# Raw weight tiles in a pool of their own, in the place of later token sums, and one more staging tile

## The chip, the cores and the metric

One core of one Trainium2 chip runs the whole step. The metric is the device time of one execution in microseconds (us). Before the change it is 3220.15 us, the median of two runs (3218.65 and 3221.65).

## The reference

One layer of a streaming encoder, for a prompt of 2048 tokens and a sample of 32 tokens, width 1024. A row-normalised input is multiplied by `w_in` (1024 by 9760), whose columns are cut into attention q, k, v and its gate, the state-space parts z, x, B, C and dt, and two merge gates:

```python
h = _rms_norm(x, pre_norm_w)
proj = h @ w_in
q, k, v, g_att, z, xbc, dt_raw, gate_a, gate_s = _split_cols(proj)
# windowed attention over q, k, v -> att; conv, SiLU and chunked scan over xbc, dt, z -> yz
branch_a = (att * jax.nn.silu(g_att)) @ w_attn_o
branch_s = yz @ w_ssm_o
merged = jax.nn.sigmoid(gate_a) * branch_a + jax.nn.sigmoid(gate_s) * branch_s
out = merged @ w_out
return x + _rms_norm(out, post_norm_w), ...
```

All of it is float32. The returned values are the two outputs and the new caches and states.

## The kernel before

**Tokens and precision.** The prompt is worked in four blocks of 512 tokens; the sample rides along in block 1 (544 columns). A float32 product is made from two halves of each operand in a shorter format: a weight `w` is split into a high part (ScalarE, L142) and a remainder (VectorE, L143), and likewise the tokens, and three products hi·hi, hi·lo, lo·hi are accumulated on TensorE (`group`, L178).

**Weights.** A weight tile holds 512 rows by 128 columns. In block 0 it comes raw from its matrix (`load_raws`, L121, 256 KB) into a pool of `NR` = 4 tiles, is split by `alloc` into one of nine `w` tiles (1 + 1 instructions of ScalarE and VectorE), and the split pair is stored to a scratch tensor `wd` (L147, 512 KB). Blocks 1 to 3 load the split pair from there (L131). `supply` runs `alloc` up to eight entries ahead of TensorE's use. A raw tile may be loaded again when `rawdone` has been moved on, which happens in `alloc` by `en["free"]` tiles at a time.

**Jobs.** A job is a pair of 128-column outputs. For the columns of x, B, C and z ("plain" pairs) block 0 makes four weight tiles and each frees its raw tile by itself. The pairs of k, v, q, the attention gate and the two merge gates ("fast" pairs, in this order: K, V, q0, g0, q1, g1, the fourth part of the state-space output, q2, g2, q3, g3, four of gate S, four of gate A) use seven products instead of eight in blocks 1 to 3. For that, block 0 makes four sums of the raw tiles on GpSimd (L136, each written over one of its inputs), splits and stores them too, although block 0 itself doesn't multiply by them. So a fast pair in block 0 has four raw tiles, eight splits and seven stores, and `free` is 0 for all of it but the last sum, which frees all four raw tiles at once. Behind the fast pairs come the attention output (ao, 8 jobs) and the output matrix (ou, 8 jobs).

**Running a job in block 0.** `emit_both` (L236 on) runs 24 matmuls for each of the two output halves into the two banks of one PSUM tile, then copies the half to a staging tile (L251, mostly `xq`, two buffers, of ScalarE's work). In the built program the first matmul of the second half waits for the copy of the first half.

**What sets the order.** The code is recorded in the order of its calls, and a scheduler with its own time estimates then orders each engine's instructions; every engine, SP's DMA queue too, works its list strictly in order. SP issues the kernel's DMAs: raw loads (L121), stores (L147), loads of split weights (L131), x (L369), z to and from scratch (L570, L696) and the scan's decay rows (L600, L603).

**Token sums.** The tiles t2, t3 and t4 (operands of the seven products) are first written by `sums_c`, at the end of block 0 for block 1. Before the change they stand in the pool `hp` from the start of the program.

Of the kernel before, what the change touches and what calls it, by code (L numbers as in the profile page):

```python
# [7 lines left out]
F32 = mybir.dt.float32  # L8
F32R = mybir.dt.float32r
# [5 lines left out]
P = 128  # L15
# [7 lines left out]
HK = KT // 2  # L23
# [4 lines left out]
C_Z, C_X, C_DT, C_GA, C_GS = 2560, 4608, 7680, 7712, 8736  # L28
CUT = object()
NW = 9  # L30
NR = 4


@with_exitstack
def hybrid_step_kernel(ctx: ExitStack, tc: tile.TileContext, ins, outs):
# [4 lines left out]
    pool = lambda n, b, **k: ctx.enter_context(tc.tile_pool(name=n, bufs=b, **k))  # L40
    const = pool("const", 1)
    wp = pool("wp", NW)
    hp = pool("hp", 1)
    up = pool("up", 2)
    sp = pool("sp", 8)
    s2 = pool("s2", 6)
    xq = pool("xq", 2)
    sm = pool("sm", 4)
    dram = pool("dram", 2, space=bass.MemoryType.DRAM)
    wdram = pool("wdram", 1, space=bass.MemoryType.DRAM)  # L50
# [24 lines left out]
    cdec = const.tile([P, 160], F32, name="cdec")  # L75
    HN = UW // 2
    hb = {n: hp.tile([P, 2, HK, UW], F32R, name=n) for n in ("h1", "h2")}
    hb.update({n: hp.tile([P, 2, HK, HN], F32R, name=n) for n in ("t2", "t3", "t4")})
    HOME = {"b11": ("h1", 0), "b12": ("h1", 1), "t1": ("h1", 1), "b21": ("h2", 0), "b22": ("h2", 1),
            "t2": ("t2", 0), "t3": ("t3", 0), "t4": ("t4", 0)}  # L80

# [27 lines left out]
    rawlist = []  # L109
    rawtiles = {}  # L110
    rawnext, rawdone = [0], [0]
# [4 lines left out]
    def load_raws():  # L116
        while rawnext[0] < min(len(rawlist), rawdone[0] + NR):
            i = rawnext[0]
            view, k0, c0 = rawlist[i]
            r = wp.tile([P, HK * P], F32, name="raw", bufs=NR)  # L120
            dma(r.rearrange("p (k c) -> p k c", k=HK), view[:, k0:k0 + HK, c0:c0 + P])  # L121
            rawtiles[i] = r
            rawnext[0] += 1

    def alloc(e):
        en = entries[e]
        w = slots[e] = wp.tile([P, 2, HK * P], F32R, name="w")
        mix = en["kind"] == "mix"
        if en["load"]:
            n = 1 if mix else 2  # L130
            dma(w[:, :n].bitcast(F32), held[en["key"]])  # L131
            return
        r = rawtiles[en["raw"]]
        if en.get("sum"):
            dst, x, y, op = en["sum"]
            pl.tensor_tensor(*(rawtiles[en["raw0"] + i] for i in (dst, x, y)), op=op)  # L136
        if mix:
            r, h = (t.rearrange("p (k c) -> p k c", k=HK) for t in (r, w[:, 0]))
            act.activation(h, r, AF.Copy)
            vec.tensor_tensor(h[:, :, 32:64], r[:, :, :32], h[:, :, :32].bitcast(F32), op=ALU.subtract)  # L140
        else:
            act.activation(w[:, 0], r, AF.Copy)  # L142
            vec.tensor_tensor(w[:, 1], r, w[:, 0].bitcast(F32), op=ALU.subtract)  # L143
        if en["keep"]:
            u = w[:, :1] if mix else w
            held[en["key"]] = wdram.tile([P, u.shape[1], HK * P], F32, name=f"wd{e}")
            dma(held[en["key"]], u.bitcast(F32))  # L147
        rawdone[0] += en["free"]
        load_raws()
# [194 lines left out]
    def block(b):  # L344
# [13 lines left out]
        def stage_a(io):  # L358
# [31 lines left out]
            def raw(name):  # L390
                j, half = dict(b11=(0, 0), b12=(0, 1), b21=(1, 0), b22=(1, 1))[name]
                return st["rawh"][j][:, :, half * (tb // 2):(half + 1) * (tb // 2)]

            def parts(name, src):
                o = operand(name, tb // 2)
                act.activation(o[:, 0], raw(src), AF.Copy)
                vec.tensor_tensor(o[:, 1], raw(src), o[:, 0].bitcast(F32), op=ALU.subtract)

            def to(dst, x, y):
                vec.tensor_tensor(raw(dst), raw(x), raw(y), op=ALU.subtract)  # L400
# [15 lines left out]
                    dma(st["t1d"][:, :, k, :nh], t[:, :, :nh].bitcast(F32))  # L416

            def sums_c():
                to("b21", "b21", "b22")
                parts("t3", "b12")  # L420
                parts("t2", "b22")
                parts("t4", "b21")
# [852 lines left out]
    for slot in blocks[0]["stage_a"](ph):  # L1275
        for f in slot:
            f()

    load_raws()
    par = const.tile([P, 208], F32, name="par")  # L1280
    convw = par[:, :96].rearrange("p (t n) -> p t n", t=4)
# [137 lines left out]

    if phase:  # L1420
        phase.pop("cm").__exit__(None, None, None)


_INS = ['x_prompt', 'x_sample', 'cache_k', 'cache_v', 'state_conv', 'state_ssm', 'pre_norm_w', 'w_in', 'conv_w', 'conv_b',
# [47 lines left out]
```

## Time and profile before

| | |
|---|---|
| median of two runs | 3220.15 us |
| the profiled execution | 3225.96 us |
| its span, first to last instruction | 3224.2 us |
| TensorE (PE) busy in it | 3009.6 us, 93% |
| VectorE (DVE) / ScalarE (ACT) / GpSimd (POOL) busy | 60% / 38% / 19% |
| DMA, mean share of 16 engines | 72.6% |
| TensorE's mean granted clock | 0.973 of full speed |

The profile lists instructions by source line. "Idle before, releaser" is the time an engine stood before an instruction and what ended it. A granted clock of 1.0 is 2.4 GHz and 0.5 is 1.2 GHz; a value between them is a mix over the stretch. A busy TensorE can be a slow one, so clock and busy time are read together.

### The profile page before, as it was taken

The page shows a single profiled execution, that of the slowest core. Times are in us where ns is not written, and L with a number is a line of the kernel's source. Part 1 is how long each engine was busy: PE and PEld are TensorE (multiplying, and loading weights), DVE is VectorE, ACT ScalarE, POOL GpSimd, SP SyncE. Part 2 cuts the span into 40 slices and gives each one's busy share as a digit, 9 for nine tenths or more (in the row PEclk, how much of TensorE's full clock was granted, in tenths as well). Part 3 has the DMA queues.
Part 4 walks back from the last instruction along what each step waited for, and adds up shares of the span by engine and source line. Part 5 has one row for each costly group of instructions (what it writes and reads, how often), then busy time and mean ns, then how long its engine had stood idle before and what let it go on. Part 6 is the DMA issues. An engine that isn't in the chain of part 4 may idle for free.

```text
span 3224.2 us, 51384 instructions
## 1 busy us (share of the span) xinstructions
PE 3009.6 (93%) x19007; PEld 2570.8 (80%) x19007; DVE 1935.7 (60%) x3965; ACT 1227.0 (38%) x2942; POOL 617.3 (19%) x698
## 2 busy tenths in 40 slices
PE   7999978887999999899999998999999999999998
PEld 6777756666899899888998777788888777788887
DVE  7788856764566666556345665556536575655622
ACT  5565434553444542124224444214313444313411
POOL 1233232322113322100011232210010222210000
PEclk9999988898999999999999999999999999999999
DMA  8888866577976676766867776686887667686794
GB/s 293 296 279 273 270 231 243 211 258 283 310 226 213 183 211 191 262 206 192 305 218 216 216 214 201 219 303 184 269 279 232 212 209 212 206 295 213 223 324 140
DMA packets 430947, 767.39 MB, mean 238 GB/s; under 512 B 35848, under 2 KB 259432, under 8 KB 430696
## 3 DMA queue, kind: packets, MB, share of 16 engines
q1 hardware_dynamic: 430696, 764.10, 72.6%
q8 instruction: 151, 2.47, 0.3%
q14 instruction: 100, 0.82, 0.1%
HBM read 587.19 MB, written 176.80 MB: 237 GB/s over the span
## 4 chain that ended last, share of the span: by engine, by line
PE 61%; DVE 12%; DMA 10%; ACT 6%; POOL 5%; issue 5%; SPq 1%; DVEq 0%; POOLq 0%; ACTq 0%
PE mm L178 51%; DMA rr<-cd 4%; POOL raw L136 2%; ACT rr L628 2%; DVE u L552 2%; DVE w L143 2%; DMA raw<-in_w_in_dram 2%; PE sd L933 1%; PE sd L659 1%; POOL rr L625 1%; PE sd L976 1%; PE sd L655 1%; PE sd L959 1%; DMA s<-zd 1%; PE sd L663 1%
## 5 line engine op out<-in xcount | busy, mean ns | idle before, releaser
L178 PE MATMUL mm<-h,w 128*128 128x512 f32 (+2 forms) x8336 | 1602.4, 346 | 104.7 <-ACT xq L251 54.6
L178 PEld LDWEIGHTS mm<-h,w 128*128 128x128 f32 x8336 | 1317.3, 193 | 324.4 <-ACT xq L251 69.3
L178 PE MATMUL mm<-v,w 128*128 128x512 f32 (+1 forms) x2400 | 487.6, 356 | 9.3 <-ACT w L142 3.7
L178 PEld LDWEIGHTS mm<-v,w 128*128 128x128 f32 x2400 | 393.3, 190 | 79.3 <-ACT w L142 4.6
L143 DVE TENSOR_TENSOR w<-raw,w 128x512 fp32r<-128x512 f32 x288 | 238.0, 841 | 96.6 <-ACT w L142 91.9
L178 PE MATMUL mm<-t,w 128*128 128x256 f32 (+1 forms) x1944 | 271.2, 287 | 0.0
L178 PEld LDWEIGHTS mm<-t,w 128*128 128x128 f32 x1944 | 249.2, 190 | 4.4 <-issue 4.3
L142 ACT ACTIVATE w<-raw 128x512 fp32r<-128x512 f32 x288 | 174.6, 627 | 157.8 <-POOL raw L136 79.6
L628 ACT ACTIVATE rr<-rr,ncum 128x128 f32<-128x128 f32 (+1 forms) x544 | 168.7, 385 | 131.7 <-POOL rr L625 131.7
L251 ACT COPY xq<-mm 128x512 f32<-128x512 f32 (+1 forms) x226 | 110.9, 508 | 232.1 <-PE mm L178 231.8
L552 DVE SCALAR_TENSOR_TENSOR u<-xq,par,u 128x512 f32<-128x512 f32 x192 | 157.8, 822 | 37.6 <-ACT u L543 36.4
L178 PE MATMUL mm<-tA,w 128*128 128x512 f32 (+2 forms) x688 | 174.6, 341 | 0.0
L914 ACT ACTIVATE pt<-sd,nm 128x192 f32<-128x192 f32 (+3 forms) x260 | 104.9, 412 | 162.2 <-DVE nm L908 157.3
L625 POOL TENSOR_SCALAR_AFFINE_SELECT rr<-rr 128x1024 f32<-128x1024 f32 (+1 forms) x68 | 87.6, 1289 | 338.8 <-DMA rr<-cd 278.4
L814 POOL TENSOR_TENSOR s<-s,cs 128x512 f32<-128x512 f32 (+1 forms) x40 | 63.9, 1606 | 454.6 <-DVE s L812 330.8
L136 POOL TENSOR_TENSOR raw<-raw 128x512 f32<-128x512 f32 x72 | 104.3, 1448 | 199.7 <-DVE w L143 195.6
L178 PEld LDWEIGHTS mm<-tA,w 128*128 128x128 f32 x688 | 118.3, 188 | 13.7 <-ACT v L1083 0.2
L178 PE MATMUL mm<-S,w 128*128 128x512 f32 (+2 forms) x344 | 115.9, 337 | 0.1
L906 DVE TENSOR_REDUCE mx<-sd 128x2 f32<-128x384 f32 (+3 forms) x140 | 66.0, 510 | 82.9 <-PE sd L933 78.2
L645 DVE SCALAR_TENSOR_TENSOR rr<-rr,sd 128x1024 f32<-128x1024 f32 (+1 forms) x68 | 79.3, 1165 | 53.0 <-ACT rr L628 53.0
L639 POOL TENSOR_TENSOR s<-xd,te 128x512 f32<-128x512 f32 (+1 forms) x68 | 76.4, 1124 | 163.1 <-DVE xd L636 163.1
L644 POOL TENSOR_TENSOR xl<-s,xh 128x512 fp32r<-128x512 f32 (+1 forms) x68 | 92.2, 1358 | 80.3 <-ACT xh L643 79.5
(274 smaller groups left out, 3788.4 us busy)
## 6 DMA issues: line engine op xcount, KB each, us to landing
w<-wd SPq DMA_DIRECT2D x810, 512.0 KB
wd<-w SPq DMA_DIRECT2D x270, 512.0 KB
raw<-in_w_in_dram SPq DMA_DIRECT2D x154, 256.0 KB
rr<-cd SPq DMA_DIRECT2D x64, 512.0 KB
ee<-cd SPq DMA_DIRECT2D x128, 128.0 KB
x<-in_x_prompt_dram SPq DMA_DIRECT2D x24, 512.0 KB
zd<-xq SPq DMA_DIRECT2D x48, 256.0 KB
s<-zd SPq DMA_DIRECT2D x48, 256.0 KB
```

The source lines that it names most:

```text
L136: pl.tensor_tensor(*(rawtiles[en["raw0"] + i] for i in (dst, x, y)), op=op)
L142: act.activation(w[:, 0], r, AF.Copy)
L143: vec.tensor_tensor(w[:, 1], r, w[:, 0].bitcast(F32), op=ALU.subtract)
L178: last_mm[0] = pe.matmul(ps, a[:, k, :], r(k, n0, n), start=start and k == 0 and i == 0, stop=stop and k == HK - 1 and i == len(ops) - 1)
L251: act.copy(y[:, n0:n0 + n], ps)
L552: vec.scalar_tensor_tensor(o[:, d0:d0 + n], src[:, t:t + n], convw[:, t, ci:ci + 1], o[:, d0:d0 + n], op0=ALU.mult, op1=ALU.add)
L625: pl.affine_select(w[:q, :, :q], w[:q, :, :q], pattern=[[0, 8], [1, q]], compare_op=ALU.is_ge, fill=-1e30, base=0, channel_multiplier=-1)
L628: act.activation(w[:q, h, :q], w[:q, h, :q], AF.Exp, scale=1.0, bias=ncum[:q, co + g * 8 + h:co + g * 8 + h + 1])
L639: pl.tensor_tensor(xe[:q].rearrange("p (h d) -> p h d", h=8), xd[:q], te[:q, hs].unsqueeze(2).broadcast_to([q, 8, 64]), op=ALU.mult)
L644: pl.tensor_tensor(xl[:q], xe[:q], xh[:q].bitcast(F32), op=ALU.subtract)
L645: vec.scalar_tensor_tensor(w[:q, :, :q], w[:q, :, :q], 0.25, pb[:q, P:P + q].unsqueeze(1).broadcast_to([q, 8, q]), op0=ALU.mult, op1=ALU.mult)
L914: act.activation(dst, src, AF.Exp, bias=nm[:, i:i + 1], scale=0.125, accum_out=den[:, i:i + 1])
```

## The change

The raw tiles get a pool of their own, `early`, with `NR` = 12 buffers, at the other end of the on-chip memory ("right"). `open_sums`, called at the head of `sums_c`, closes it when the last raw tile has been used and opens the pool `late` in its place, which holds t2, t3 and t4. The staging pool `xq` goes from two to three buffers. No instruction of the computation is added or removed.

```diff
-NR = 4
+NR = 12
...
-    xq = pool("xq", 2)
+    xq = pool("xq", 3)
+    early_cm = tc.tile_pool(name="early", bufs=NR, side="right")
+    early = early_cm.__enter__()
...
-    hb.update({n: hp.tile([P, 2, HK, HN], F32R, name=n) for n in ("t2", "t3", "t4")})
+    late_cm = []
+
+    def open_sums():
+        if not late_cm:
+            assert rawnext[0] == rawdone[0] == len(rawlist)
+            early_cm.__exit__(None, None, None)
+            late_cm.append(tc.tile_pool(name="late", bufs=1, side="right"))
+            p = late_cm[0].__enter__()
+            hb.update({n: p.tile([P, 2, HK, HN], F32R, name=n) for n in ("t2", "t3", "t4")})
...
         while rawnext[0] < min(len(rawlist), rawdone[0] + NR):
             i = rawnext[0]
             view, k0, c0 = rawlist[i]
-            r = wp.tile([P, HK * P], F32, name="raw", bufs=NR)
+            r = early.tile([P, HK * P], F32, name="raw")
...
             def sums_c():
+                open_sums()
                 to("b21", "b21", "b22")
...
     if phase:
         phase.pop("cm").__exit__(None, None, None)
+    late_cm[0].__exit__(None, None, None)
```

The scheduler lays block 0 out anew; behind the first part of block 1 every engine's list is the one of before. In the rows below numbers behind a name are those of single buffers, and line numbers of the changed kernel are up to twelve higher (L121 is L131 there, L142 is L152, L251 is L261, L782 is L793, L147 is L157, L369 is L379).

On ScalarE, in the pairs of gate A, before: `mm_6677` is the PSUM tile of one pair, `w_6596`, `w_6601`, `w_6633` and `w_6636` are its four weight tiles, and the four `w` rows behind them are splits of its sums.

```order
L142 ACTIVATE w_6596<-raw_6555 128x512
L142 ACTIVATE w_6601<-raw_6557 128x512
L142 ACTIVATE w_6633<-raw_6559 128x512
L142 ACTIVATE w_6636<-raw_6561 128x512
L370 ACTIVATE xn_7445,ss_7446<-x_7444 128x1024
L142 ACTIVATE w_6641<-raw_6561 128x512
L142 ACTIVATE w_6647<-raw_6559 128x512
L142 ACTIVATE w_6653<-raw_6555 128x512
L142 ACTIVATE w_6659<-raw_6557 128x512
L251 COPY xq_6676<-mm_6677 128x512
L782 ACTIVATE tA_6713<-xq_6676 128x512
L251 COPY xq_6676<-mm_6677 128x512
```

The same place after the change: `mm_6693` is the PSUM tile of a pair, and the raw tiles 6465 to 6471 are those of the pair behind it.

```order
L152 ACTIVATE w_6718<-raw_6465 128x512
L793 ACTIVATE tA_6690<-xq_6586 128x512
L152 ACTIVATE w_6723<-raw_6467 128x512
L152 ACTIVATE w_6755<-raw_6469 128x512
L261 COPY xq_6692<-mm_6693 128x512
L152 ACTIVATE w_6758<-raw_6471 128x512
L793 ACTIVATE tA_6729<-xq_6692 128x512
L152 ACTIVATE w_6763<-raw_6471 128x512
L152 ACTIVATE w_6769<-raw_6469 128x512
L152 ACTIVATE w_6775<-raw_6465 128x512
L152 ACTIVATE w_6781<-raw_6467 128x512
L261 COPY xq_6692<-mm_6693 128x512
```

Before, all eight splits of a pair stood ahead of that pair's two copies; now the eight splits between a pair's copies belong to the next pair, and three of them stand ahead of the first copy, one and then four behind it.

On SP, at the same pairs, before: the loads of x for block 1 (L369) stand among the raw loads.

```order
L121 DMA raw<-in_w_in_dram 128x4x128 x4
L369 DMA x<-in_x_prompt_dram 128x1024
L147 DMA wd_6705<-w 128x1024
L147 DMA wd_6710<-w 128x1024
L147 DMA wd_6745<-w 128x1024
L147 DMA wd_6751<-w 128x1024
L147 DMA wd_6757<-w 128x1024
L147 DMA wd_6763<-w 128x1024
L147 DMA wd_6769<-w 128x1024
L121 DMA raw<-in_w_in_dram 128x4x128 x4
```

After, x is loaded at the end of block 0, among the last stores of the output matrix:

```order
L131 DMA raw<-in_w_out_dram 128x4x128
L157 DMA wd_7320<-w 128x1024
L157 DMA wd_7325<-w 128x1024
L157 DMA wd_7362<-w 128x1024
L157 DMA wd_7367<-w 128x1024
L375 DMA nw<-in_pre_norm_w_dram 128x1024
L379 DMA x<-in_x_prompt_dram 128x1024
L157 DMA wd_7439<-w 128x1024
L157 DMA wd_7444<-w 128x1024
L379 DMA x<-in_x_prompt_dram 128x1024
```

Five loads of x and one of the norm's weights have moved from the fast pairs to behind all raw loads, eight stores from the end of block 0. On TensorE the five groups of transposes that need them stood ahead of matmuls 1, 25, 49, 73 and 151 of the 192 of the output matrix, and now stand behind 120, 142, 153, 170 and 190 of them. At the program's start SP issues twelve raw loads instead of four ahead of the small constants.

## Rows read from the trace of the kernel before

**Rows 1.** Busy time by stretch: us, each engine, granted clock (PEclk), DMA share, GB/s.

```profile
50.00:403.00 353.00, 338.25 (x1738) 270.93 (x1736) 290.06 (x469) 192.53 (x410) 102.64 (x106) 0.99 0.85 280
403.00:429.00 26.00, 24.03 (x108) 18.35 (x108) 13.84 (x28) 7.81 (x13) 9.13 (x8) 1.00 0.65 225
429.00:516.00 87.00, 60.31 (x197) 44.43 (x198) 46.29 (x61) 29.58 (x53) 31.07 (x22) 0.82 0.63 227
516.00:683.00 167.00, 150.13 (x848) 108.07 (x846) 125.44 (x297) 93.70 (x278) 48.85 (x32) 0.93 0.63 230
683.00:785.00 102.00, 77.13 (x273) 57.41 (x269) 49.66 (x72) 40.59 (x70) 29.65 (x22) 0.87 0.75 269
785.00:882.00 97.00, 97.00 (x454) 79.39 (x454) 54.57 (x99) 42.38 (x74) 15.61 (x11) 1.00 0.92 315
882.00:3224.20 2342.20, 2229.65 (x15257) 1965.21 (x15255) 1321.09 (x2853) 794.09 (x2001) 376.87 (x480) 0.98 0.71 227
```

**Rows 2.** What TensorE waited for from 403 to 785 us: total, times, longest.

```profile
PE mm L178 <- ACT xq L251: 27.2, 10, 5.5
PE mm L178 <- ACT w L142: 20.0, 13, 2.3
PE mm L178 <- DVE w L143: 5.4, 2, 2.7
```

**Rows 3.** TensorE in order of time: start, length, instructions, [idle before and releaser].

```profile
726.70 6.08 PE L178 MATMUL mm<-h,w 128*128 128x512 f32 x24 [1.85 <-ACT w L142]
736.52 7.13 PE L178 MATMUL mm<-h,w 128*128 128x512 f32 x24 [3.74 <-ACT xq L251]
745.51 0.74 PE L178 MATMUL mm<-h,w 128*128 128x512 f32 x2 [1.85 <-ACT w L142]
```

**Rows 4.** ScalarE in the same stretch, in order of time.

```profile
726.03 2.18 ACT L142 ACTIVATE w<-raw 128x512 fp32r<-128x512 f32 x4
...
735.37 0.63 ACT L142 ACTIVATE w<-raw 128x512 fp32r<-128x512 f32 x1 [1.04 <-POOL raw L136]
735.90 0.57 ACT L251 COPY xq<-mm 128x512 f32<-128x512 f32 x1
```

**Rows 5.** SP's DMA issues in the same stretch, in order of time.

```profile
727.39 9.67 SPq L147 DMA_DIRECT2D wd<-w  x7
737.16 2.90 SPq L121 DMA_DIRECT2D raw<-in_w_in_dram  x4
```

**Rows 6.** Two short stretches of the cycle before, columns as in Rows 1.

```profile
718.00:725.00 7.00, 6.84 (x23) 5.08 (x21) 2.03 (x6) 0.18 (x2) 0.00 (x0) 0.76 1.04 329
725.50:728.00 2.50, 1.30 (x5) 0.80 (x6) 1.33 (x3) 2.50 (x5) 0.00 (x0) 1.00 0.05 18
```

**Rows 7.** The page's DMA issues: count and size of each.

```profile
wd<-w SPq DMA_DIRECT2D x270, 512.0 KB
raw<-in_w_in_dram SPq DMA_DIRECT2D x154, 256.0 KB
```

**Rows 8.** TensorE in the attention output's jobs, unbroken and at full clock.

```profile
799.08 2.95 PE L178 MATMUL mm<-u,w 128*128 128x512 f32 x12
801.87 2.95 PE L178 MATMUL mm<-v,w 128*128 128x512 f32 x12
```

**Rows 9.** VectorE: four splits without and four with GpSimd's sums beside them.

```profile
726.67 2.50 DVE L143 TENSOR_TENSOR w<-raw,w 128x512 fp32r<-128x512 f32 x4 [6.47 <-ACT w L142]
...
731.30 5.42 DVE L143 TENSOR_TENSOR w<-raw,w 128x512 fp32r<-128x512 f32 x4 [0.49 <-ACT w L142]
```

**Rows 10.** TensorE's waits from 882 us to the end, first row.

```profile
PE mm L178 <- ACT xq L251: 25.3, 15, 3.9
```

**Rows 11.** GpSimd's waits from 882 us to the end, for a staging tile.

```profile
POOL xq L541 <- DMA zd<-xq: 24.5, 7, 6.0
```

**Rows 12.** SP's queue at the start: the last small constant.

```profile
15.73 0.43 SPq L63 DMA_DIRECT2D dbc<-in_d_skip_dram  x1
```

**Rows 13.** TensorE at the start: the first use of a small constant.

```profile
28.91 0.27 PE L1302 MATMUL sd<-cst,s 120*128 120x120 f32 x1
```

## What I predicted, before the result was known

> **What bounds the kernel now.** I read the busy times by stretch first, since a share over the whole program hides where time is lost. In [rows 1] TensorE is all but full nearly everywhere: 338 of 353 us up to the fast pairs, 97 of 97 us in the jobs behind them, 2230 of 2342 us in blocks 1 to 3. The hole is at the fast pairs of block 0: from 429 to 516 us it works 60 of 87 us at a clock of 0.82, from 683 to 785 us 77 of 102 us at 0.87. Between them, where attention runs beside the pairs, it works 150 of 167 us at 0.93. No other engine is full there, and the DMA engines are busy 0.63 to 0.75 of the time. So a chain of waits, and no engine, sets the pace.
>
> The list of waits names it [rows 2]: TensorE waits for the copies out of PSUM (L251, 27.2 us) and for splits of weights (L142 and L143, 25.4 us). One cycle in order of time shows why. A first half starts at 726.70, the second at 736.52, the next pair's first at 745.51 [rows 3]: 18.8 us a pair. The four splits that the first half needs start at 726.03, so only then were the raw tiles there [rows 4]. Then come the sums on GpSimd, whose last split starts at 735.37, and only behind it stands the copy of the first half, at 735.90, while that half had ended at 732.8: 3.7 us lost. The four raw loads of the next pair stand on SP behind all seven stores, at 737.16 [rows 5], because the last sum frees all four raw tiles at once. They land while TensorE runs its second half, and 1.85 us are lost again before the next splits are done. The DMA engines run full while stores and raw loads drain (share 1.04, 329 GB/s) and then stand still, share 0.05, until the next stores come [rows 6]. Two more losses ride on it: the 24 matmuls take 6.08 and 7.13 us [rows 3], and at full clock they take 5.58 us, as 12 of them go by in 801.87 − 799.08 = 2.79 us [rows 8].
>
> **The change, part by part.** *Twelve raw tiles.* They hold three fast pairs instead of one. The raw tiles of the next pair are then loaded long before they are wanted, and its splits can be made during the pair before, which is what the new order of ScalarE's list does. What is left as a limit for a pair is the largest of these:
> - TensorE: 48 matmuls at 2.79/12 us, 11.15 us [rows 8], and one handover to the copy; 11.9 us with 0.7 us for it, a copy's own 0.57 us [rows 4] and a little.
> - DMA: four loads of 256 KB and seven stores of 512 KB [rows 7], 4.72 MB. At 329 GB/s, the rate measured while the same mix drains [rows 6], 14.3 us. At the mean rate of the stretch, 269 GB/s [rows 1], 17.5 us.
> - VectorE: eight splits, of which four took 2.50 us and the four beside the sums 5.42 us [rows 9], 7.9 us, plus what the pair's outputs need. Not the limit where no attention runs.
>
> I take 14.3 us: it comes from a row in which the engines really had both kinds of transfers waiting. The bounds are 11.9 and 17.5 us.
>
> The Trainium skill (DMA: Bandwidth & Descriptors, "Where 436 GB/s comes from") gives about 358 GB/s as one core's share of the memory; by it the pair would take 13.2 us, and the sum below would gain another 10 us. The 329 GB/s of the rows is below that.
>
> Now the stretches. From 429 to 516 us there are four pairs: 4 × 14.3 = 57.2 us instead of 87, −30. From 683 to 785 us there are 102/18.8 = 5.4 pairs: 77.6 us, −24. K and V, from 403 to 429 us, already take 13 us each at full clock [rows 1], 0. From 516 to 683 us TensorE's 150 us at a clock of 0.93 are 140 us at full clock; VectorE's 125 us must fit in too. With the share of waiting of the first stretch (353/338) it would be 146 us; I take 150, since VectorE would then be busy 84% of it in an order fixed beforehand: −17. Bounds 146 and 167. Together −71.
>
> *The order of the earlier part of block 0.* The plain pairs free their raw tiles one by one and leave 15 us of 353 to win [rows 1]; I take −1, and 0 to −10 as bounds.
>
> *The third staging tile.* In blocks 1 to 3 the lists are unchanged, so it only takes waits away. GpSimd waited 24.5 us for a staging tile whose z was still being stored [rows 11], which delays ScalarE and so part of the 25.3 us that TensorE waits for copies [rows 10]. In the cases that I followed the copy stood behind exponentials of the scan, which a staging tile doesn't help. I take −2; bounds 0 and −20.
>
> *The start.* Eight more raw loads, 2.1 MB, go ahead of the small constants: at 329 GB/s these come 6.4 us later. The last was issued at 15.73 us [rows 12], and TensorE's first use of one is at 28.91 us [rows 13], so about 6 us of cover remain: 0. Without that cover it would cost the 6.4 us.
>
> *The end of block 0.* The loads of x are issued behind 24 of the 32 stores of the last two matrices. Splits run up to eight weight tiles ahead, so that is when the output matrix begins, 120 matmuls or 28 us ahead of the first transpose, so the transposes should not wait. But the last of them now stands 2 matmuls instead of 42 ahead of block 1's first job: up to 9.8 us of cover is gone from the chain that makes the first operands. The scheduler has put the first two operands earlier, so I take +2, bounds 0 and +10. The pool `late` opens when the last raw tile has long been split: 0.
>
> The sum is −72 us, made against the profiled execution of 3225.96 us. That run lies 5.8 us above the median; the same loss taken from the median gives 3220 − 72 = **3148 us**. With 13 to 16 us a pair, and 146 to 160 us in the middle, it is 3132 to 3174 us.
>
> **The rivals.** *The DMA engines are the wall already.* From 683 to 785 us the engines are busy 0.75 of the time and move 269 GB/s [rows 1]. If that were all this mix gives, a pair would take 17.5 us: −17 in the first stretch, −8 in the last, and with −17 in the middle the kernel takes 3179 us. Against it speaks the still stretch of 0.05 between two full ones [rows 6].
>
> *VectorE and GpSimd are in each other's way.* Four splits took 2.50 us alone and 5.42 us beside the sums [rows 9]. Where attention runs, VectorE has 125 us of work in 167; packed tighter, more of it meets GpSimd and the middle gains nothing: 3165 us. The Trainium skill (SBUF — State Buffer, "Who interferes with whom") has a rule for it: a VectorE instruction with two inputs in SBUF contends with a GpSimd instruction that reads there. These two rows agree.
>
> *The split ahead blocks the copy: slower than before.* A weight tile is free only when its store has landed, and there are still nine. The splits that now stand ahead of a copy on ScalarE belong to the next pair and wait for such landings; before, they belonged to the own pair. If a store lands as late as seven of them take at 329 GB/s, 11.2 us, each half takes that long, and with 1.85 us between pairs one takes 24.3 us: +10 in the first stretch, +29 in the last, 3259 us. It decides once a store lands more than half a pair's 14.3 us after its issue. Against it: four raw loads issued behind seven stores at 737.16 us [rows 5] were there within 8 us.
>
> *It changes nothing* would need a limit of nine weight tiles that holds the splits back as much as the raw tiles did. The new order splits one pair ahead with these nine, so I count it with the first rival.
>
> **How the numbers follow.** Forecast 0.58, the DMA wall 0.20, VectorE 0.17, slower 0.05. About 2%, 64 us, is what a measurement of this kernel can tell from no change, so faster means below 3156 us. Most of the forecast's own range lies below that, little of the first two rivals' does: faster 0.55, same 0.41, slower 0.04. The range, 3115 to 3190 us, takes in both rivals on this side; below, it reaches to pairs of 11.9 us (−23 us more) with ten more from the staging tile and the plain pairs.
>
> **What would show it.** Raw loads should no longer be named among ScalarE's waits in the fast pairs. From the start of q0 to the start of the attention output there should be about 285 us instead of 356, with a granted clock above 0.95 and a DMA share above 0.85. A pair without attention should take 13 to 15 us. If ScalarE's splits wait for stores and TensorE for copies, the third rival is at work; if the pairs take 17 us with a share near 1, the first. A wait of TensorE for x at the end of block 0 over 10 us, or blocks 1 to 3 changed by more than 20 us, would show that I mis-sized the small terms.

## The result, and the profile after

The changed kernel takes 3137.6 us (median of two runs) against 3220.15 us: a ratio of 0.974, 95% interval [0.970, 0.979]. In a second measurement, with five runs of it and nine of the kernel before, it was 3145.5 us and a ratio of 0.977 [0.975, 0.979], 73 us of 3219. The profiled execution has a span of 3135.8 us, 88.4 less than before.

Busy times by stretch; the seven lines answer line by line to those of [rows 1]: up to K's first matmul, K and V, the four fast pairs q0 to g1, the attention stretch (state output of group 3, q2 to g3 and the first of the next pairs), the last pairs, the attention output with the output matrix, blocks 1 to 3. The columns are the same. The last line of [rows 1] begins 3.7 us behind block 1's first matmul, which stood at 878.3 us; the last line here begins with it.

```profile
50.00:398.40 348.40, 334.95 (x1738) 268.71 (x1736) 283.99 (x465) 191.03 (x408) 102.08 (x104) 1.00 0.86 287
398.40:428.40 30.00, 25.73 (x106) 19.89 (x106) 23.30 (x36) 11.58 (x20) 17.16 (x13) 0.89 0.72 231
428.40:484.50 56.10, 48.24 (x200) 37.35 (x200) 44.03 (x56) 26.04 (x46) 31.07 (x21) 0.97 0.88 317
484.50:648.30 163.80, 146.76 (x849) 106.57 (x847) 130.13 (x302) 97.09 (x285) 51.98 (x36) 0.94 0.73 256
648.30:711.60 63.30, 62.77 (x272) 49.99 (x269) 39.21 (x46) 34.27 (x60) 25.22 (x19) 1.00 1.01 358
711.60:805.90 94.30, 93.00 (x421) 74.85 (x420) 46.22 (x107) 37.27 (x68) 13.27 (x8) 1.00 0.81 286
805.90:3135.80 2329.90, 2225.49 (x15286) 1962.04 (x15284) 1334.54 (x2866) 800.63 (x2011) 381.30 (x483) 0.99 0.72 230
```

Read down the first number of each line. The gain lies in the third and the fifth: 87 to 56 us, and 102 to 63 us, where TensorE now works 62.8 of 63.3 us at full clock. The attention stretch hardly moved: 167 to 164 us, with the clock still at 0.94 and VectorE busier than before, 130 us instead of 125. K and V became slower, 26 to 30 us.

What TensorE waited for from 398 to 712 us, for [rows 2] (total, times, longest):

```profile
PE mm L188 <- ACT xq L261: 11.3, 4, 5.0
PE sd L964 <- DVE s L823: 3.6, 1, 3.6
PE sd L866 <- ACT xq L261: 3.5, 1, 3.5
PE mm L188 <- ACT w L152: 3.3, 2, 1.9
```

The 25 us of waits for splits of weights have shrunk to 3.3 us. ScalarE, which made those splits, no longer waits for any raw load between 428 and 712 us; before, that was 15.4 us on ten occasions for w_in alone. Copies out of PSUM (L261) are still waited for: of the 11.3 us in the first row 10.8 lie in the attention stretch.

TensorE in order of time, for [rows 3]: K's second half and V behind it, two starts of pairs in the first fast stretch, then the last stretch (start, length, instructions, idle time before and what ended it).

```profile
409.65 19.66 PE L188 MATMUL mm<-h,w 128*128 128x512 f32 x74 [2.62 <-ACT kr L261]
...
452.64 0.72 PE L188 MATMUL mm<-h,w 128*128 128x512 f32 x2 [1.36 <-ACT w L152]
...
466.38 0.73 PE L188 MATMUL mm<-h,w 128*128 128x512 f32 x2 [1.89 <-ACT w L152]
...
661.17 43.92 PE L188 MATMUL mm<-h,w 128*128 128x512 f32 x188 [0.53 <-ACT xq L261]
```

From 452.64 to 466.38 us a pair takes 13.7 us; before, the four pairs of that stretch took 87 us, 21.8 each. In the last stretch 188 matmuls run without a gap, so a pair takes 43.92 × 48/188 = 11.2 us instead of 18.8, which is TensorE's own time by [rows 8].

### The profile page after: what moved, and what is told of

Read it like the earlier page. It is cut to its first block, busy times and chain, and to the rows that moved or that the text cites. A ratio compares the mean times of both kernels' runs of the same rounds, so it can differ in the third digit from the quotient of the medians.

```text
span 3135.8 us, 51395 instructions
## 1 busy us (share of the span) xinstructions
PE 2969.5 (95%) x19007; PEld 2546.0 (81%) x19007; DVE 1937.1 (62%) x3965; ACT 1224.9 (39%) x2942; POOL 624.7 (20%) x698
## 4 chain that ended last, share of the span: by engine, by line
PE 58%; DVE 10%; DMA 8%; issue 6%; ACT 5%; POOL 4%; SPq 1%; POOLq 0%; DVEq 0%; ACTq 0%
PE mm L188 49%; DMA rr<-cd 3%; POOL raw L146 2%; ACT rr L639 2%; DVE u L563 1%; PE sd L987 1%; PE sd L670 1%; PE sd L944 1%; DMA s<-zd 1%; PE sd L666 1%; POOL rr L636 1%; PE sd L970 1%; DMA ee<-cd 1%; PE sd L674 1%; ACT pt L925 1%
## 5 line engine op out<-in xcount | busy, mean ns | idle before, releaser
L188 PE MATMUL mm<-h,w 128*128 128x512 f32 (+2 forms) x8336 | 1566.8, 342 | 66.2 <-ACT xq L261 35.6
L188 PEld LDWEIGHTS mm<-h,w 128*128 128x128 f32 x8336 | 1294.3, 191 | 271.2 <-ACT xq L261 49.7
L188 PE MATMUL mm<-v,w 128*128 128x512 f32 (+1 forms) x2400 | 483.8, 355 | 4.6 <-DVE S L779 1.5
L188 PEld LDWEIGHTS mm<-v,w 128*128 128x128 f32 x2400 | 391.1, 189 | 72.7 <-issue 4.2
L153 DVE TENSOR_TENSOR w<-raw,w 128x512 fp32r<-128x512 f32 x288 | 229.4, 810 | 93.7 <-ACT w L152 85.6
L188 PE MATMUL mm<-t,w 128*128 128x256 f32 (+1 forms) x1944 | 271.5, 287 | 0.0
L188 PEld LDWEIGHTS mm<-t,w 128*128 128x128 f32 x1944 | 249.7, 190 | 4.2 <-issue 4.2
L152 ACT ACTIVATE w<-raw 128x512 fp32r<-128x512 f32 x288 | 176.9, 632 | 156.6 <-PE mm L188 73.2
L639 ACT ACTIVATE rr<-rr,ncum 128x128 f32<-128x128 f32 (+1 forms) x544 | 168.0, 385 | 118.7 <-POOL rr L636 118.6
L261 ACT COPY xq<-mm 128x512 f32<-128x512 f32 (+1 forms) x226 | 111.1, 509 | 193.4 <-PE mm L188 192.9
L188 PE MATMUL mm<-tA,w 128*128 128x512 f32 (+2 forms) x688 | 174.1, 340 | 0.0
L188 PEld LDWEIGHTS mm<-tA,w 128*128 128x128 f32 x688 | 118.4, 188 | 14.6 <-ACT v L1094 0.2
L188 PE MATMUL mm<-S,w 128*128 128x512 f32 (+2 forms) x344 | 116.9, 340 | 0.2 <-DVE S L1082 0.2
```

The costliest lines, as they stand in the source:

```text
L188: last_mm[0] = pe.matmul(ps, a[:, k, :], r(k, n0, n), start=start and k == 0 and i == 0, stop=stop and k == HK - 1 and i == len(ops) - 1)
L261: act.copy(y[:, n0:n0 + n], ps)
L639: act.activation(w[:q, h, :q], w[:q, h, :q], AF.Exp, scale=1.0, bias=ncum[:q, co + g * 8 + h:co + g * 8 + h + 1])
```

## The experiments

All twelve ran beside the kernel before, in three groups of four. The table gives the ratio to it with its 95% interval, the median, and five stretches of the profiled execution, in us, read from TensorE's rows in order of time. The stretches are cut at marks that every kernel has: K's first matmul, the first transpose of V, the first matmul of the state output of group 3, the last transpose of attention, block 1's first matmul, the end. "Raw" and "xq" are the numbers of raw and staging tiles.

| kernel | raw, xq, sums on | ratio | median | K, V | q0 to g1 | attention | last pairs to block 1 | blocks 1 to 3 |
|---|---|---|---|---|---|---|---|---|
| before | 4, 2, GpSimd | 1 | 3220.2 | 24.8 | 87.7 | 167.6 | 195.0 | 2345.9 |
| changed | 12, 3, GpSimd | 0.974 [0.970, 0.979] | 3137.6 | 30.7 | 55.4 | 163.8 | 157.5 | 2329.9 |
| e7_again (the changed kernel) | 12, 3, GpSimd | 0.977 [0.975, 0.979] | 3145.5 | 31.0 | 55.5 | 165.5 | 158.0 | 2345.2 |
| e1_xq2 | 12, 2, GpSimd | 0.980 [0.978, 0.982] | 3148.9 | 30.7 | 55.5 | 165.5 | 156.8 | 2348.7 |
| e2_nr4_xq3 | 4, 3, GpSimd | 0.999 [0.997, 1.000] | 3211.4 | 24.7 | 85.0 | 168.1 | 198.3 | 2329.3 |
| e3_place | 4, 2, GpSimd | 1.002 [1.001, 1.003] | 3222.1 | 24.4 | 85.1 | 168.0 | 197.7 | 2336.8 |
| e4_nr8 | 8, 3, GpSimd | 0.978 [0.976, 0.979] | 3142.8 | 27.6 | 53.9 | 164.4 | 155.5 | 2344.5 |
| e5_sums_dve | 12, 3, VectorE | 0.968 [0.966, 0.970] | 3111.6 | 24.6 | 49.1 | 142.3 | 154.1 | 2340.5 |
| e6_sums_tiny | 12, 3, GpSimd, 16 columns | 0.966 [0.964, 0.968] | 3110.2 | 25.7 | 46.3 | 143.3 | 155.5 | 2339.7 |
| e8_store_more | 12, 3, GpSimd | 0.984 [0.982, 0.986] | 3166.7 | 34.1 | 55.8 | 158.1 | 178.6 | 2338.7 |
| e9_dummy | 12, 3, VectorE | 0.977 [0.973, 0.982] | 3147.8 | 29.4 | 64.3 | 159.0 | 159.2 | 2336.0 |
| e10_before_dve | 4, 2, VectorE | 0.980 [0.976, 0.984] | 3156.8 | 23.8 | 68.7 | 142.8 | 176.4 | 2347.5 |
| e11_dve_nr8 | 8, 3, VectorE | 0.967 [0.962, 0.972] | 3116.4 | 25.9 | 47.3 | 143.0 | 156.5 | 2344.2 |
| e12_dve_more | 12, 3, VectorE | 0.973 [0.967, 0.979] | 3136.5 | 28.2 | 50.9 | 143.0 | 173.9 | 2341.3 |

The last column moves by 15 us between two executions of the very same kernel (changed and e7_again), so a few us in it mean nothing; the columns of block 0 repeat within 2 us.

One thing has to be known of all these kernels: the scheduler sets the order of every engine's list again for each of them. By their profiles e3 has the lists of the kernel before; e2 differs from it, and e9 from e5, in GpSimd's list alone. In the others the order on ScalarE and VectorE moved too, a little in e1 and in many places in the rest, so such a run measures its edit and a new order together.

### Which count of tiles gave what

**e1_xq2**, the third staging tile taken away:

```
-    xq = pool("xq", 3)
+    xq = pool("xq", 2)
```

> The changed kernel with two staging tiles instead of three; twelve raw tiles stay. Theory (the raw tiles gave what block 0 gained, the third staging tile what blocks 1 to 3 gained, about 16 us): block 1 begins at 806 us as in the changed kernel, blocks 1 to 3 take 2342 to 2346 us again as before the change, the whole about 3152 us. Rival (blocks 1 to 3 gained from the new order at the end of block 0 or from the new place of the tiles): 3138 to 3141 us, blocks 1 to 3 stay at 2330 us. A third outcome, that fast pairs in block 0 need the third tile because copies come closer together: block 1 begins 10 us or more later than 806 us.

**e2_nr4_xq3**, the eight further raw tiles taken away:

```
-NR = 12
+NR = 4
```

> The changed kernel with four raw tiles instead of twelve; the third staging tile stays. Theory: the fast pairs of block 0 fall back to 18 us or more each (87 us for q0 to g1, about 100 us for the last stretch) and block 1 begins at about 878 us; only blocks 1 to 3 keep their gain, so about 3204 us. Rival (part of block 0's gain came from the third staging tile, since a copy must find one free): block 1 begins before 870 us and the whole takes 3190 us or less.

**e3_place**, both edits of e1 and e2, so that only the pool and the place are new:

> Four raw tiles and two staging tiles as before the change, but the raw tiles in their own pool whose place the token sums take over. Both theories that give all the gain to the counts of tiles expect 3220 us, within 4 us of the kernel before. If the place itself or the order that goes with it (loads of x behind the last raw loads) gives or costs something, it shows here: 3210 us or less, or 3230 us or more.

**e7_again**, no edit:

> The changed kernel itself once more, beside the other runs of this call, so that they have a common base. Twelve raw tiles alone gave 0.980 of the time before, the third staging tile 0.9965; if the two simply multiply, 0.977, about 3142 us. If they help each other, 0.974 or less.

Of the two counts block 0 depends on the raw tiles alone: 55.5 us from q0 to g1 with twelve of them and two staging tiles, 85 us with four and three. e2 against e3, in one group, puts the third staging tile at 3222.1 − 3211.4 = 10.7 us, and their intervals do not meet; e1 against e7 gives 0.3% too, from two groups whose intervals overlap. So it is worth about 11 us, and not the 16 us that the two profiles differ by in blocks 1 to 3: e7 shows 2345.2 us there with three tiles, as much as before with two. The two profiled executions of the changed kernel differ in TensorE's clock (mean 0.99 and 0.98 in that stretch); the first was a lucky one. What the tile takes away can be seen among GpSimd's waits. With two tiles (this row is of e1_xq2, as [rows 11] of before) it waits for z to be stored; with three no such row is left:

```profile
POOL xq L552 <- DMA zd<-xq: 25.4, 7, 7.5
```

e7's result is the plain product of the two parts, 0.977; they do not help each other. e3 came out 0.2% above the kernel before, although every engine has the same instructions in the same order. I found no cause for it in the profile; it stays open, and differences of that size between other kernels should be read with it in mind.

**e4_nr8**, eight raw tiles:

```
-NR = 12
+NR = 8
```

> The changed kernel with eight raw tiles, so two fast pairs instead of three. Theory (a pair needs only the raw tiles of the next pair while its own are summed): within 5 us of the changed kernel, 3138 to 3143 us, 14 to 15 us a pair from q0 to g1. Rival (the depth counts, since the sums free four tiles at once and the stores stand ahead of the loads on SP's queue): 16 us or more a pair, ScalarE waits for raw loads again, 3155 us or more.

3142.8 us, no difference from the changed kernel that can be measured. The last pairs alone, from the last transpose of attention to the last matmul of a fast pair, take 64.0 us, and 64.4 in e7. One pair of tiles in advance does all that TensorE can use while GpSimd makes the sums.

### What holds the attention stretch

**e5_sums_dve**, the sums of weights on the other engine:

```
-            pl.tensor_tensor(*(rawtiles[en["raw0"] + i] for i in (dst, x, y)), op=op)
+            vec.tensor_tensor(*(rawtiles[en["raw0"] + i] for i in (dst, x, y)), op=op)
```

> The changed kernel with the token-independent sums of weights (four per fast pair) on VectorE instead of GpSimd. Theory (GpSimd's sums slow VectorE down in the attention stretch, and the splits wait for them): VectorE loses about 20 us of slowed work there and takes on 16 sums of 0.68 us, the stretch from the state output of group 3 to the last turned attention tile falls from 164 us to 150 to 156, the whole is about 3128 us. Rival (the copies stand behind exponentials and splits in an order fixed beforehand, whoever makes the sums): the stretch stays at 161 to 168 us, the whole at 3136 to 3145 us.

**e6_sums_tiny**, which leaves out all but 16 of the 512 columns of each sum:

```
-            pl.tensor_tensor(*(rawtiles[en["raw0"] + i] for i in (dst, x, y)), op=op)
+            pl.tensor_tensor(*(rawtiles[en["raw0"] + i][:, :16] for i in (dst, x, y)), op=op)
```

> The changed kernel with the sums of weights made over 16 of 512 columns only, so the weights for blocks 1 to 3 are not the right ones; every instruction and its order stay. GpSimd's load and the time that a split waits for a sum are all but taken away. Theory (GpSimd's sums are what keeps the attention stretch at 164 us): it falls to 152 us or less, the whole to 3125 us or less, and the pairs without attention stay at 11.5 to 14 us. Rival (the fixed order): the stretch stays above 160 us.

Both bring the attention stretch from 164 to 142 or 143 us, more than the theory asked for, and e5 makes a whole kernel of 3111.6 us, the fastest of those that compute everything. But the order changed in both, in e6 too, where the expectation has it stay: ScalarE's list is another one. Taken by themselves they don't part the sums from the order. The rows of e5, in the order first fast pairs, attention, last pairs:

```profile
420.70:470.40 49.70, 46.24 (x200) 36.18 (x199) 44.93 (x71) 26.53 (x46) 9.35 (x6) 1.00 1.04 374
470.40:612.70 142.30, 140.01 (x850) 102.16 (x849) 127.38 (x330) 95.17 (x283) 7.05 (x4) 1.00 0.81 284
612.70:675.00 62.30, 61.62 (x268) 49.21 (x265) 40.43 (x63) 33.93 (x60) 0.31 (x2) 1.00 1.03 371
```

In the attention stretch TensorE now works 140.0 of 142.3 us at a clock of 1.00. VectorE has taken on 30 sums and is still busy for less time than in the changed kernel, 127.4 us against 130.1. Where that comes from is seen in its instructions there. First the changed kernel, then e5 (busy time, mean ns of one):

```profile
L153 DVE TENSOR_TENSOR w<-raw,w 128x512 fp32r<-128x512 f32 x68 | 50.9, 763 | 17.7 <-ACT w L152 15.9 <-DMA wd<-w 1.5
L921 DVE TENSOR_TENSOR es<-nm,sks 128x4 f32<-128x4 f32 x16 | 7.5, 466 | 0.2
L919 DVE SCALAR_TENSOR_TENSOR nm<-mx,sks 128x4 f32<-128x4 f32 x16 | 5.9, 369 | 0.1
L146 POOL TENSOR_TENSOR raw<-raw 128x512 f32<-128x512 f32 x32 | 46.0, 1437 | 90.8 <-DVE w L153 60.0 <-DMA wd<-w 24.8 <-DVE es L921 4.0
```

```profile
L153 DVE TENSOR_TENSOR w<-raw,w 128x512 fp32r<-128x512 f32 x66 | 44.0, 684 | 3.3 <-ACT w L152 2.8
L146 DVE TENSOR_TENSOR raw<-raw 128x512 f32<-128x512 f32 x30 | 20.6, 687 | 0.2
L919 DVE SCALAR_TENSOR_TENSOR nm<-mx,sks 128x4 f32<-128x4 f32 x16 | 2.5, 156 | 0.1
L921 DVE TENSOR_TENSOR es<-nm,sks 128x4 f32<-128x4 f32 x16 | 2.5, 155 | 0.1
```

A VectorE instruction over four columns takes 155 ns, and with GpSimd's sums about it 466 ns on average. That is not work but standing still until the other engine's instruction is through. In the changed kernel five of the sixteen lay beside a sum and took 0.86 to 1.23 us; the other eleven took 0.15 to 0.17. And it is passed on. ScalarE's exponentials wait for these small instructions, and the copy that TensorE waits for stands behind the exponentials. Three views of the changed kernel in order of time, VectorE, GpSimd and then ScalarE:

```profile
568.25 1.21 DVE L153 TENSOR_TENSOR w<-raw,w 128x512 fp32r<-128x512 f32 x1 [0.68 <-ACT w L152]
569.38 1.22 DVE L921 TENSOR_TENSOR es<-nm,sks 128x4 f32<-128x4 f32 x1
```

```profile
568.98 1.59 POOL L146 TENSOR_TENSOR raw<-raw 128x512 f32<-128x512 f32 x1
```

```profile
570.63 0.20 ACT L922 ACTIVATE es<-es 128x4 f32<-128x4 f32 x1 [1.61 <-DVE es L921]
...
571.53 0.58 ACT L261 COPY xq<-mm 128x512 f32<-128x512 f32 x1
```

The sum ends at 570.57 us and the four-column instruction at 570.60. At 572.17 us TensorE goes on, after 3.63 us of waiting for that copy. By the mean times in e5 the two VectorE instructions are 0.5 and 1.1 us too long, so 1.6 of the 3.63 us (an estimate) are theirs; ScalarE had also stood 2.26 us for a sum, up to 567.58 us.

In both experiments three things went together, then: VectorE was left alone, splits waited less for sums (in the attention stretch ScalarE waits 9.2 us for them in e5 and 22.0 in the changed kernel), and the order was another. **e9_dummy** takes the first by itself. It is e5 with a GpSimd addition of the same size beside each sum, for whose result nothing waits:

```
         if en.get("sum"):
+            pl.tensor_tensor(idle, w[:, 0].bitcast(F32), w[:, 1].bitcast(F32), op=ALU.add)
```

> The version with the sums on VectorE, and beside each of them one addition of 128x512 on GpSimd that reads the weight tile just split and writes a tile that nobody reads, so nothing waits for it; the lists of all other engines stay as they are. Theory (contention: VectorE's instructions get longer while GpSimd reads and writes SBUF): the attention stretch grows from 142 us to 152 to 160 us, and 128x4 instructions of VectorE there take 0.4 us on average instead of 0.15. Rival (latency: with the sums on GpSimd the splits waited for them, and a busy GpSimd alone does no harm): 142 to 147 us.

The attention stretch goes back from 142 to 159 us, with the lists of VectorE, ScalarE, SyncE and TensorE unchanged. Rows of e9 for the same groups, where L154 is the split, L147 the sum, L924 the four columns and L156 the added instruction:

```profile
L154 DVE TENSOR_TENSOR w<-raw,w 128x512 fp32r<-128x512 f32 x68 | 52.9, 798 | 3.1 <-ACT w L153 3.0
L147 DVE TENSOR_TENSOR raw<-raw 128x512 f32<-128x512 f32 x29 | 21.3, 734 | 0.2
L924 DVE TENSOR_TENSOR es<-nm,sks 128x4 f32<-128x4 f32 x16 | 5.8, 359 | 0.1
L156 POOL TENSOR_TENSOR idle<-w 128x512 f32<-128x512 f32 x29 | 45.7, 1574 | 95.0 <-DVE w L154 56.3 <-DVE es L924 24.1 <-DVE nm L922 14.0
```

VectorE's busy time rises from 127.4 to 145.9 us for the same instructions, 18.5 us; the stretch grows by 16.7 us. Three of the sixteen four-column instructions lay beside an addition and took 1.23 to 1.27 us, the other thirteen 0.15 to 0.16. So contention alone, with the order of e5, gives back 16.7 of the 21.5 us between e5 and the changed kernel. From q0 to g1 it is 15 us longer too, but 64.3 us are 9 more than in the changed kernel, so for that stretch e9 doesn't tell what the sums cost there. What is not told apart either: in e9 VectorE also carries the sums, which makes it fuller (92% busy) than in the changed kernel, GpSimd's rotary products stand behind the additions, and a weight tile is held until its addition has read it. How much of the changed kernel's 21 us was the splits' waiting for slow sums, or the order, is therefore open.

**e10_before_dve**, the kernel before with nothing but the sums moved (the same edit as e5, at its L136):

> The kernel before (four raw tiles, two staging tiles) with the sums on VectorE. Theory (two separate limits: the raw tiles freed at once, and GpSimd's sums): the sums alone shorten the chain of a pair a little, q0 to g1 from 87 us to 70 to 80 us, the attention stretch by 5 to 12 us, the whole 3180 to 3200 us, well above the 3112 us with twelve raw tiles. Rival (GpSimd's sums were the whole trouble and twelve raw tiles only hid it): 3150 us or less.

Here the theory's figures missed: it expected 3180 us or more, and the kernel took 3156.8, all but what the rival asked for. Moving the sums is worth 63 us to the kernel before, as much as the eight further raw tiles are (e1, 0.980 too). The two overlap and do not replace each other: with both it is 3111.6 us. Attention takes 142.8 us with four raw tiles as with twelve. The pairs without attention do need the tiles. The end of e10's last stretch on TensorE:

```profile
683.99 6.10 PE L178 MATMUL mm<-h,w 128*128 128x512 f32 x24 [1.86 <-ACT w L142]
690.76 5.83 PE L178 MATMUL mm<-h,w 128*128 128x512 f32 x24 [0.68 <-ACT xq L251]
698.45 6.10 PE L178 MATMUL mm<-h,w 128*128 128x512 f32 x24 [1.86 <-ACT w L142]
```

A pair takes 698.45 − 683.99 = 14.5 us, and each still begins by waiting for its splits. Yet ScalarE waits for no raw load from 632 to 714 us. It comes to the splits at 697.79 us straight from its work on the last copy of the pair before (L782, at 697.25). So what the number of raw tiles changes here is the place of the splits in ScalarE's list.

### What the DMA engines allow

**e8_store_more**, one kept weight of each fast pair stored twice:

```
             dma(held[en["key"]], u.bitcast(F32))
+            if en.get("sum") and en["key"][1] == "s1":
+                dma(wdram.tile([P, 2, HK * P], F32, name=f"we{e}"), u.bitcast(F32))
```

> The changed kernel with one of the seven kept weights of each fast pair of block 0 stored twice, so 5.24 MB a pair instead of 4.72. Theory (the DMA engines at about 360 GB/s are the limit of a pair wherever the twelve raw tiles are used up): 1.4 us more per pair, q0 to g1 6 us longer, the last stretch 63 to 71 us, the whole 12 to 14 us slower. Rival (TensorE sets the pace of the pairs and the 360 GB/s are only what it asks for): 0 to 3 us slower.

**e12_dve_more**, the same lines in e5:

> The version with the sums on VectorE, with one of the seven kept weights of each fast pair stored twice. Theory (with the sums off GpSimd the DMA engines are the next limit of the pairs without attention: 374 GB/s at a share of 1.04 from q0 to g1): q0 to g1 grows by 4 to 6 us from 49 us, the last stretch and the attention output together by 15 to 30 us, as with the sums on GpSimd. Rival (there is room on the DMA engines): under 3 us in either.

e8 is 21 us slower than e7, which neither side expected. From q0 to g1 nothing changes (55.8 us) although the DMA engines move 337 GB/s there and 316 in e7, and in e12 the same stretch takes 50.9 us at 383 GB/s. So the DMA engines had room where the theory saw their limit. What is lost comes after the attention stretch, 20.6 us (the attention stretch is 7 us shorter; I have not traced why), and late. The last stretch of e8, in two parts, then TensorE at the start of two pairs and ScalarE ahead of the second (its L190, L152 and L263 are the lines L188, L152 and L261 of the changed kernel):

```profile
646.10:690.00 43.90, 40.28 (x168) 31.04 (x168) 25.17 (x30) 22.15 (x38) 16.82 (x12) 1.00 0.95 339
690.00:725.00 35.00, 27.73 (x101) 20.59 (x102) 13.85 (x18) 15.26 (x28) 11.66 (x10) 0.90 0.92 333
```

```profile
690.69 7.38 PE L190 MATMUL mm<-h,w 128*128 128x512 f32 x24 [1.86 <-ACT w L152]
...
707.95 7.34 PE L190 MATMUL mm<-h,w 128*128 128x512 f32 x24 [3.37 <-ACT w L152]
```

```profile
705.60 0.57 ACT L263 COPY xq<-mm 128x512 f32<-128x512 f32 x1
...
706.74 2.72 ACT L152 ACTIVATE w<-raw 128x512 fp32r<-128x512 f32 x5
```

Up to 690 us the pairs run nearly as in the changed kernel. Then a pair takes 707.95 − 690.69 = 17.3 us and waits for its splits, and with the waits the clock falls to 0.90. But the splits do not wait for data. From 646 to 730 us neither ScalarE nor GpSimd waits for a raw load or a store, and the DMA engines stand still from 704.0 to 704.5 us (share 0.00), 2 us before the splits begin. The splits of the next pair stand behind both copies of the pair before, as in the kernel before the change: with the added stores the scheduler laid the last pairs out in the old order. e12 shows the same: 2 us from q0 to g1, 20 us at the end, and there too a pair's splits stand behind the copies of the pair before (677.23 us, behind a copy at 676.07) with no wait for a raw load. So in the last pairs these two runs show what that order costs: about 11 of the 20.6 us of e8. The other 9 are lost in the two matrices behind the pairs, where TensorE waits 4.5 us once for rows of x (L386); the rest of them is not traced. Whether the last pairs would reach a limit of the DMA engines in the order of the changed kernel is not shown.

What the changed kernel itself issues from 648.3 to 711.6 us:

```profile
wd<-w SPq DMA_DIRECT2D x33, 512.0 KB
raw<-in_w_attn_o_dram SPq DMA_DIRECT2D x14, 256.0 KB
raw<-in_w_in_dram SPq DMA_DIRECT2D x8, 256.0 KB
```

That is 23.1 MB, and 358 GB/s over 63.3 us moved 22.7. The 22 raw loads are as many as 5.5 pairs use, so the twelve raw tiles leave the stretch as full as they came into it.

**e11_dve_nr8**, e5 with eight raw tiles:

> The version with the sums on VectorE and eight raw tiles instead of twelve, three staging tiles. Theory (the raw tiles in advance, 3.1 MB in twelve, carry the last stretch past the DMA engines' limit): with eight 1 MB less is there, the last stretch is 3 us longer at about 360 GB/s, the whole 3112 to 3118 us. Rival (eight are as good): 3112 us within 2. Rival (the pairs now come so fast that eight run dry): 3125 us or more.

The last pairs alone take 62.4 us in e11 and in e5, where the theory wanted 3 us more; the stretch up to block 1 is 2.4 us longer (156.5 and 154.1 us), all of it behind those pairs. So 1 MB less in advance costs the last pairs nothing. The whole, 0.967 [0.962, 0.972] against 0.968 [0.966, 0.970], tells neither from the other.

## Why the prediction was right, and where its steps were wrong

The forecast was 3148 us and the range 3115 to 3190 us; it took 3137.6, and 3145.5 when measured again. The main reading held: the pairs without attention ran at the pace of a chain of waits that hung on the number of raw tiles, and more of them broke it (e1 and e2).

**How the raw tiles held the chain.** The prediction read from the splits' start at 726.03 us that only then the raw tiles were there [rows 4]. The rows don't say so much. ScalarE came to these splits without a pause, from its work on the last copy of the pair before, and from 683 to 783 us it waited for a raw load once (first its instruction ahead of the splits, then its wait in the kernel before):

```profile
725.49 0.63 ACT L782 ACTIVATE tA<-xq 128x512 f32<-128x512 f32 x1
```

```profile
ACT w L142 <- DMA raw<-in_w_in_dram: 2.0, 1, 2.0
```

The DMA share was 0.64 from 725.0 to 725.5 us, 0.21 in the next half microsecond and 0.01 in the one behind, so the loads landed at about that time too. Which of the two would have come last is not shown. What is shown is that twelve raw tiles let the scheduler put the next pair's splits ahead, and that the old order makes TensorE wait even where ScalarE waits for no raw load (17.3 us a pair in e8, 14.5 in e10).

The terms of the sum were off, some by more than half, and they made up for each other:

- **q0 to g1: −30 forecast, −32 measured, for the wrong reason.** A pair takes 13.7 us, close to the 14.3 worked out from 329 GB/s. But the DMA engines were not the limit: their share was 0.88, and without GpSimd's sums the same pairs take 49.1 us, at 374 GB/s (e5). GpSimd's sums held them, and the step on the limits of a pair named TensorE, the DMA engines and VectorE, and not GpSimd. ScalarE waited 15.7 us for sums there; how much of the 6 us is that waiting and how much contention is open.
- **The last stretch: −24 forecast, −38 measured.** The step took 14.3 us a pair there too, from a rate in a row of 7 us that was no ceiling: 358 GB/s flow here at a share of 1.01, and 371 in e5. And less had to be moved: 23.1 MB were issued, where 5.4 pairs of 4.72 MB are 25.5, since only 33 stores fall into the stretch. What remains is TensorE's own pace, 11.2 us a pair, busy 62.8 of 63.3 us. That is below the step's lower bound of 11.9 us, whose handover of 0.7 us to the copy is gone as well. The Trainium skill (DMA: Bandwidth & Descriptors, "Where 436 GB/s comes from") gives about 358 GB/s as one core's limit to its memory. The 358 GB/s of this stretch are no such limit here: e5 moves 371 in the same stretch, and e12 383 from q0 to g1.
- **The attention stretch: −17 forecast, −4 measured.** Here the rival with VectorE and GpSimd in each other's way was right, for most of it by e9, and the forecast wrong. The forecast counted VectorE's 125 us as work that fits into 150 us. Some 20 us of it was standing still for GpSimd, handed on to the exponentials and copies in a fixed order: in e10 the same instructions take 124.2 − 19.2 = 105 us, where 19.2 us are the sums that VectorE has there in addition. TensorE's 140 us at full clock, which the step worked out, are what it does in e5, once the sums are gone. The rule in the Trainium skill (SBUF — State Buffer, "Who interferes with whom") says that the two engines share a pair of ports by an exclusive lock, and that a VectorE instruction with two inputs in SBUF contends for it with a GpSimd instruction that reads SBUF. e9 agrees: the four-column subtractions, of two small tiles in SBUF, go from 155 to 359 ns on average, while the products of L991, with one input in PSUM, take 280 ns in the changed kernel, 282 ns in e5 and 279 ns in e9.
- **K and V: 0 forecast, +6 measured.** The step put nothing here. This is the mechanism of the rival that ended slower, the split ahead that blocks the copy, in small and with another cause. TensorE waits 1.65 us for GpSimd (L718) and then 2.62 us for the copy of K's first half (the row at 409.65 us above). That copy, at 409.03 us, stands on ScalarE behind two splits that wait for GpSimd's sums, 4.29 us for the first. The clock is at 0.89 in the stretch, and the 74 matmuls take 19.66 us instead of 17.44 in e5. With the sums on VectorE K and V are back at 24.6 us. The same happens at the transposes of V, where the next stretch begins: 3.5 us for a copy, behind a split that waits 2.85 us. Waits of ScalarE for stores to land, which the rival had named, are all but absent (0.6 us from 428 to 712 us).
- **The third staging tile: −2 forecast, about −11 measured** (e2 against e3), inside the bounds given, but not the value taken from them. The step put GpSimd's 24.5 us aside because the copies that it followed stood behind exponentials. Part of TensorE's wait for copies in blocks 1 to 3 did go: 22.5 us in e3, 16.9 in e2. The rest I have not traced.
- **The small terms held.** The plain pairs and the start together gave 5 us (−1 and 0 forecast; bounds 0 and −10). The end of block 0 cost 1 us (+2 forecast), and the longest wait of a transpose for x is 1.1 us. The pool `late` cost nothing that shows.

Of the signs named in advance, 283 us from q0 to the attention output (285 forecast), the raw loads gone from ScalarE's waits, and the small wait for x came as told. A granted clock above 0.95 and a DMA share above 0.85 came in the stretches without attention and not in the one with it (0.94 and 0.73), and that is where the sum was too hopeful. By the sum of the profiled executions, 6 − 32 − 4 − 38 − 5 − 16 + 1 = −88 us. Blocks 1 to 3 take 15 us longer in e7, the same kernel; with that execution in its place about 73 us remain, as in the second measurement.

## What to carry to other kernels

When a chain of waits is broken by more buffers, list every engine that the chain runs through as the next limit, the slow helper too. Where a scheduler sets the order, compare each engine's list before and after: an edit to a transfer or to an engine can move the order too, and the run then measures both. Work moved to GpSimd to spare VectorE isn't free for VectorE: compare the length of its smallest instructions with and without GpSimd beside them, and price the move by that. Here VectorE did 30 sums itself in 20.6 us and was done sooner than when GpSimd did 32 of them in 46.0.

## What the runs showed of the hardware

A VectorE instruction over 128x4 elements (L921) took 155 ns alone (e5) and up to 1.23 us beside a GpSimd addition of 128x512 in the changed kernel, which itself took 1.44 us on average; the same addition took 0.69 us on VectorE (e5). The slowdown was not in proportion to the data moved: an instruction of almost no data lost as much time as a full one, or more (in the rows above 1.22 us instead of 0.16, and 1.21 instead of 0.68). The DMA engines moved 371 GB/s over a stretch of 62 us (e5) at a share of 1.03 and 383 GB/s over 51 us (e12) at a share of 1.05, while 329 GB/s at a share of 1.04 were seen over 7 us in the kernel before [rows 6]; what makes the rate differ at like shares was not tried.
